# Five channels of a depthwise convolution: the running sum in a PSUM bank instead of SBUF

## The chip, the cores and the metric

The kernel runs on one core of a Trainium2 chip. The core has five engines with a queue each, which run in order and wait for each other through semaphores: TensorE (PE in the profile) multiplies matrices into PSUM, VectorE (DVE) and ScalarE (ACT) work on SBUF and PSUM, GpSimd (POOL) works on SBUF, SyncE (SP) starts most transfers. PSUM is used here as eight banks of 128 partitions by 512 float32 numbers. The metric is the device time of one execution in microseconds (us); before the change it is 1309.3 us, the median of three runs (1308.62 to 1310.32).

## The reference, cut to what matters

A decoder layer on 512 tokens of 1024 features: half of a feed-forward layer, a mixer of attention and convolution, the second half of the feed-forward, and an embedding under a gate. What the change touches is the mixer's convolution branch:

```python
x = x + 0.5 * swiglu(rmsnorm(x, ffn1_norm[i]), ffn1_wgu[i], ffn1_wdown[i])
h = rmsnorm(x, mix_norm[i])
z = h @ w_in[i]
...
a = sliding_window_attention(q, k, v, sinks[i]) @ attn_proj[i]
ca, cb = jnp.split(zc, 2, axis=-1)
u = ca * jax.nn.sigmoid(cb)
u = causal_depthwise_conv(u, dw_w[i], dw_b[i])     # 31 taps, each channel by itself
c = jax.nn.silu(layernorm(u, conv_ln_g[i], conv_ln_b[i])) @ conv_proj[i]
merged = jax.nn.sigmoid(ga) * a + jax.nn.sigmoid(gb) * c
x = x + merged @ w_out[i]
```

For every channel, y[t] = b + the sum over d = 0 to 30 of w[30 − d] · u[t − d].

## The kernel before, in words

Activations lie as [feature, token] tiles of 128 × 512 in float32; the 1024 features are eight such tiles. Every large product is made of float32 operands split into a high and a low part, so each 128 × 128 block of weights costs three matmuls (`mm3`, L113 to L115). A weight arrives as a piece of 512 KB on SyncE's queue; ScalarE rounds it to the high part `whi` (L88) and VectorE subtracts to get `wlo` (L89; for the gates GpSimd does).

The mixer's parts are issued in an order written out by hand, the string ORDER (L39 to L43): `a` and `b` are the convolution's input and gate projections (`ca`, `cb`), `A`, `E`, `V` the scores, softmax and values of one block of 128 queries and eight heads, `g` and `h` the gates' projections (`ga`, `gb`), `p` attention's projection (`ap`), `L` the convolution's norm. From this program order a scheduler makes each engine's queue ahead of time, by priorities and by its own estimate of times. `conv_gate` (L299) makes the convolution's input u (L306) and calls `conv` under `tc.high_priority(offset=-800)`, an offset that puts the taps behind other work that is ready.

"Channel c" below means a tile of 128 channels. `conv` (L311) starts y with the first tap and the bias on VectorE (L314), then adds 30 taps. For c = 0, 2 and 4 ScalarE makes each product `ct` (L322) in a ring of two buffers and GpSimd adds it to y (L323). For c = 1, 3, 5, 6 and 7 VectorE does product and addition in one instruction (L325): y, shifted by d, = u × weight + y; u, y and the weight (one number for each partition) all lie in SBUF. That makes 5 × 30 = 150 instructions in five chains. `conv_norm` (L523) then sums the eight y on GpSimd (L528, L530), takes mean and variance, and normalizes.

The eight PSUM banks are two rings: `pf_tile`, four banks, for the projections and `f_g`; `ps_tile`, 8 − NPF = four banks, for `f_u` of the feed-forward and, in the mixer, for the transposed queries (`qTp`, L411), four tiles of scores per block (`sc`, L430), the transposed probabilities (`pT`, L470), the values' output (`o`, L478), and the norms' column sums and spreads. A tile's bank is free once its last reader is done: for `sc` that is VectorE's mask-and-maximum L438, which also makes the maxima `m`; for `qTp` and `pT` ScalarE's high part (L88) and VectorE's low part (L89, `qT_l`, `p_l`); for `o` four ScalarE copies (L484). L454 is the softmax's exponential on ScalarE, L462 its scaling on GpSimd.

Of the kernel before, what the change touches and what calls it, by code (L numbers as in the profile page):

```python
# [8 lines left out]
F32 = mybir.dt.float32  # L9
# [25 lines left out]

# The order in which the mixer's parts are issued: K keys and values, Q a half of the queries;
# A scores, E softmax, V values of one block; a, b the convolution's input and its gate;
# g, h the gates' projections; p attention's projection; L the convolution's norm.
ORDER = """  # L39
# [7 lines left out]
def hybrid_layer(ctx: ExitStack, tc: tile.TileContext, a: dict, out: bass.AP):  # L47
# [9 lines left out]
    def ps_tile(name):  # L57
        return psum.tile([P, S], F32, tag="ps", name=name, bufs=8 - NPF)

    def pf_tile(name):  # L60
        return psum.tile([P, S], F32, tag="pf", name=name, bufs=NPF)

    def ftile(name):
        return act.tile([P, S], F32, tag="a", name=name, bufs=NBIG)
# [4 lines left out]
    NBIG = 60  # L69
    NPF = 4  # L70

    def ttile(name):
# [11 lines left out]

# [1 line left out]
    def split_into(hi, lo, src, scale=None, eng=nc.vector):  # L86
# [14 lines left out]
    def piece(src, eng=nc.vector):  # L101
        """A weight piece [P, n] from DRAM as its two parts."""
        n = src.shape[1]
        raw = wraw.tile([P, PIECE], F32, tag="raw", name="raw")
        hi = wspl.tile([P, PIECE], F32R, tag="hi", name="whi")
        lo = wspl.tile([P, PIECE], F32R, tag="lo", name="wlo")
        nc.sync.dma_start(raw[:, 0:n], src)
        split_into(hi[:, 0:n], lo[:, 0:n], raw[:, 0:n], eng=eng)
        return hi, lo

    def mm3(ps, w, x, start, stop):
        """ps += w.T @ x of operands in two parts."""
        nc.tensor.matmul(ps, w[1], x[0], start=start, stop=False)  # L113
        nc.tensor.matmul(ps, w[0], x[0], start=False, stop=False)  # L114
        nc.tensor.matmul(ps, w[0], x[1], start=False, stop=stop)  # L115
# [3 lines left out]

# [1 line left out]
    def rsqrt(name, v, n):  # L121
        """1/sqrt(v) of a small positive tile by Newton's iteration."""
        y = small.tile([P, n], F32, tag=f"y{n}", name=f"{name}_y", bufs=2 if n > 8 else 4)
        h = small.tile([P, n], F32, tag=f"h{n}", name=f"{name}_h", bufs=2)
        nc.vector.tensor_single_scalar(
            h.bitcast(I32), v.bitcast(I32), 1, op=ALU.logical_shift_right
        )
        nc.vector.tensor_scalar(
            y.bitcast(I32), h.bitcast(I32), -1, 0x5F3759DF, op0=ALU.mult, op1=ALU.add
        )  # L130
        nc.vector.tensor_scalar(h, v, -0.5, None, op0=ALU.mult)
        for _ in range(3):
            b = small.tile([P, n], F32, tag=f"b{n}", name=f"{name}_b", bufs=2)
            nc.vector.tensor_tensor(b, y, y, op=ALU.mult)
            nc.vector.tensor_tensor(b, b, h, op=ALU.mult)
            nc.vector.scalar_tensor_tensor(y, b, 1.5, y, op0=ALU.add, op1=ALU.mult)
        return y

    def colsum(name, acc):
        """Sums over the partitions of [P, S], tokens on partitions: [P, NT] in PSUM."""  # L140
        ps = ps_tile(f"{name}_cs")
        for t in range(NT):
            nc.tensor.matmul(
                ps[:, t : t + 1], acc[:, t * P : (t + 1) * P], ones[:, 0:1], start=True, stop=True
            )
        return ps[:, 0:NT]
# [7 lines left out]
    def spread(name, r):  # L154
        """[P, NT], tokens on partitions, to [P, S] with tokens on the free axis, on each partition."""
        dg = tmp.tile([P, NT, P], F32, tag="t", name=f"{name}_dg")
        nc.vector.tensor_tensor(
            dg,
            ident.unsqueeze(1).broadcast_to([P, NT, P]),
            r.unsqueeze(2).broadcast_to([P, NT, P]),  # L160
            op=ALU.mult,
        )
        ps = ps_tile(f"{name}_sp")
        nc.tensor.matmul(ps, ones, dg.rearrange("p t q -> p (t q)"), start=True, stop=True)
        rb = tmp.tile([P, S], F32, tag="rb", name=f"{name}_rb", bufs=3)
        nc.scalar.copy(rb, ps)
        return rb
# [16 lines left out]

# [1 line left out]
    g_all = const.tile([P, 8, KD], F32, name="g_all")  # L186
# [23 lines left out]
    def consts():  # L210
# [19 lines left out]

        # the gains of q's and k's unrotated parts are both k's
        qcs, kcs = table("qcs", gq), table("kcs", gk)
# [3 lines left out]
    def ffn(tag, wgu, wdown, h, ss, first, after):  # L236
        """x += 0.5 * swiglu; `after` takes each new tile of x."""
        rb = None
# [45 lines left out]

# [1 line left out]
    def proj(tag, w_piece, h, nk=KD, off=0, bank=None):  # L286
        """One [P, S] tile of h @ w, features on partitions."""
        ps = (bank or pf_tile)(tag)
        for k in range(nk):
            c = off + k * P  # L290
            mm3(ps, part(w_piece, slice(c, c + P)), h[k], k == 0, k == nk - 1)
        return ps
# [16 lines left out]

    # depthwise causal convolution; some channels' taps are ScalarE's and GpSimd's  # L310
    def conv(c):  # L311
        u = us[c]
        ys[c] = y = ftile(f"y{c}")
        nc.vector.tensor_scalar(  # L314
            y, u, dww[:, c, PAD:TAPS], dwb[:, c : c + 1], op0=ALU.mult, op1=ALU.add
        )
        for d in range(1, TAPS):
            wk = dww[:, c, PAD - d : TAPS - d]
            yd, ud = y[:, d:S], u[:, 0 : S - d]
            if c in (0, 2, 4):  # L320
                t = tmp.tile([P, S], F32, tag="ct", name=f"ct{c}_{d}", bufs=2)[:, 0 : S - d]
                nc.scalar.activation(t, ud, AF.Copy, scale=wk)  # L322
                nc.gpsimd.tensor_tensor(yd, yd, t, op=ALU.add)  # L323
            else:
                nc.vector.scalar_tensor_tensor(yd, ud, wk, yd, op0=ALU.mult, op1=ALU.add)  # L325

    # q, k, v with tokens on partitions
    def heads_rsqrt(tag, zs, n, scale):
        """scale / sqrt(mean of squares + EPS) of each head of each block of tokens."""
        v = small.tile([P, NT * n], F32, tag=f"hv{n}", name=f"{tag}_v", bufs=2)  # L330
# [9 lines left out]
    def rope(tag, z3, n, tab, t):  # L340
        """Gain and rotation of the rotated part of each head, in place."""
        w = tmp.tile([P, n, 16], F32, tag="rope", name=f"{tag}_w", bufs=2)
# [7 lines left out]
    def token_major(tag, pieces, kper, n):  # L350
        """h2.T @ w for each block of tokens: NT tiles in PSUM, several to a bank when they are small."""
        per = S // n
# [14 lines left out]
    kT = [rtile(f"kT{i}") for i in range(2)]  # L367
    # each part of v as [v0, 0, v1], so that a pair's heads take their own half of a column
    vp = [act.tile([P, 2, 3, HD], F32R, tag="a", name=f"v{t}", bufs=NBIG) for t in range(NT)]
# [25 lines left out]
    def queries(g):  # L395
        """Four pairs of heads (j, j + 8) of the queries, rotated; their norm and the scores' scale are in rq."""
        pss = token_major(f"q{g}_", [a["wq"][4 * g + i] for i in range(4)], 2, S)
# [11 lines left out]
    def scores(g, t):  # L409
        """Masked scores of eight heads (four pairs) of one block of queries, and their maxima."""  # L410
        pt = ps_tile(f"qTp{g}_{t}")  # L411
# [93 lines left out]
    def attn_proj(o):  # L505
        """Attention's projection under its gate."""
        if o == 0:
# [15 lines left out]
    def conv_norm():  # L523
        """Layer norm over channels, then silu."""
        acc = tmp.tile([P, S], F32, tag="acc", name="ln_acc", bufs=2)
# [48 lines left out]

# [1 line left out]
    h4, ss4, after4 = next_norm("pg", g_gate)  # L576
# [11 lines left out]

# [1 line left out]
    rb4 = None  # L590
# [31 lines left out]
def _layout(inputs):  # L622
    """The inputs as the program reads them, and tables that depend on shapes alone."""
    import numpy as np
# [6 lines left out]
    def kxn(w):  # L631
        """[K, N] -> [N/128 tiles][128 of K, K/128, 128 of N]."""
        kt, nt = w.shape[0] // P, w.shape[1] // P
        return w.reshape(kt, P, nt, P).transpose(2, 1, 0, 3).reshape(nt, P, kt * P)
# [31 lines left out]

    rows = lambda v: np.broadcast_to(v, (P, v.shape[-1]))  # noqa: E731
    gains = np.stack(
# [53 lines left out]
```

## Time and profile before

| | |
|---|---|
| median of three runs | 1309.3 us (1308.62 to 1310.32) |
| span of the profiled execution | 1306.9 us |
| TensorE busy | 1241.3 us (95%) |
| VectorE busy | 804.9 us (62%) |
| ScalarE busy | 496.8 us (38%) |
| GpSimd busy | 379.5 us (29%) |

The profile is one execution. Its page cuts the span into 40 slices of 32.7 us and gives each engine's busy share in tenths (9 is 90% or more); "PEclk" is the clock that TensorE was granted, in tenths of full speed. Groups of instructions are listed as line, engine, operation, output<-inputs, shapes, count | busy us, mean ns | idle us of the engine ahead of them and who ended it. A view of one line gives the shortest, median and longest duration in ns, and the first and last start in us. The chain of waits is followed back from the last instruction to what released each step. A shorter shape stands for a whole group: the taps' widths run from 511 down to 482. In a timeline several instructions of one kind in a row are merged, with their count.

### The profile page before, as it was taken

The numbers are of one execution on the slowest core, as the hardware profiler recorded it, in microseconds if no ns is written. First come the engines' busy times: TensorE is split into PE (matmuls) and PEld (weight loads), VectorE is DVE, ScalarE is ACT, GpSimd is POOL, SyncE is SP. The second block draws the span as 40 slices with busy tenths as digits, with TensorE's granted clock in tenths as the row PEclk, the third lists the DMA queues.
The fourth block names the chain that finished last, engine by engine and source line by source line (L and its number), as shares of the span: only waits on it lengthen the run. The fifth ranks groups of instructions, "written<-read, shape, count | busy, mean of one in ns | idle before, by whom it ended". The sixth has DMA issues, their size and how long they took to land.

```text
span 1306.9 us, 14445 instructions
## 1 busy us (share of the span) xinstructions
PE 1241.3 (95%) x5534; PEld 1015.0 (78%) x5534; DVE 804.9 (62%) x1076; ACT 496.8 (38%) x789; POOL 379.5 (29%) x322
## 2 busy tenths in 40 slices
PE   7999999999999878786889999999999999999998
PEld 5888888888888666565767878888888888888886
DVE  7544444434448988999999665575444444444447
ACT  5333333222225457563755454333333333222242
POOL 4000000011116979867687350050000000011140
PEclk9999999999999989898988999999999999999999
DMA  6223222333322212121011123232232223333331
GB/s 210 97 97 97 97 97 97 89 100 94 101 95 71 80 49 65 49 65 49 17 49 65 65 97 113 81 113 83 97 99 98 95 97 98 96 89 105 109 97 65
DMA packets 35206, 115.27 MB, mean 88 GB/s; under 512 B 4416, under 2 KB 5952, under 8 KB 35136
## 3 DMA queue, kind: packets, MB, share of 16 engines
q1 hardware_dynamic: 34992, 114.31, 27.2%
q8 instruction: 43, 0.70, 0.2%
q14 instruction: 27, 0.22, 0.1%
q10 hardware_dynamic: 144, 0.03, 0.0%
HBM read 112.23 MB, written 2.10 MB: 87 GB/s over the span
## 4 chain that ended last, share of the span: by engine, by line
PE 75%; DVE 18%; ACT 3%; POOL 2%; issue 2%; DMA 0%; SPq 0%; DVEq 0%; POOLq 0%
DVE y L325 10%; PE f_d L114 6%; PE f_d L113 6%; PE f_d L115 6%; PE f_g L115 6%; PE f_u L115 6%; PE f_g L114 6%; PE f_g L113 6%; PE f_u L114 6%; PE f_u L113 6%; DVE wlo L89 2%; POOL y L323 1%; ACT s L454 1%; PE cp L113 1%; PE wo L115 1%
## 5 line engine op out<-in xcount | busy, mean ns | idle before, releaser
L88 ACT ACTIVATE whi<-raw 128x1024 fp32r<-128x1024 f32 (+1 forms) x210 | 219.4, 1045 | 566.9 <-PE f_u L115 258.6
L89 DVE TENSOR_TENSOR wlo<-raw,whi 128x1024 fp32r<-128x1024 f32 (+1 forms) x194 | 258.1, 1331 | 240.6 <-ACT whi L88 240.5
L325 DVE SCALAR_TENSOR_TENSOR y<-u,c_dww,y 128x511 f32<-128x511 f32 (+15 forms) x150 | 171.7, 1156 | 1.4
L323 POOL TENSOR_TENSOR y<-y,ct 128x511 f32<-128x511 f32 (+14 forms) x90 | 127.3, 1415 | 35.0 <-ACT ct L322 29.5
L113 PE MATMUL f_d<-f_a_h,wlo 128*128 128x512 f32 x352 | 137.1, 390 | 0.0
L115 PE MATMUL f_d<-f_a_l,whi 128*128 128x512 f32 x352 | 137.1, 389 | 0.0
L114 PE MATMUL f_d<-f_a_h,whi 128*128 128x512 f32 x352 | 137.1, 389 | 0.0
L257 DVE TENSOR_TENSOR f_gs<-f_g,f_n_rb 128x512 f32<-128x512 f32 x44 | 30.4, 691 | 104.7 <-PE f_g L115 95.9
L322 ACT ACTIVATE ct<-u,c_dww 128x511 f32<-128x511 f32 (+14 forms) x90 | 62.4, 707 | 65.7 <-POOL y L323 65.2
L113 PEld LDWEIGHTS f_d<-f_a_h,wlo 128*128 128x128 f32 x352 | 66.1, 188 | 13.8
L115 PEld LDWEIGHTS f_d<-f_a_l,whi 128*128 128x128 f32 x352 | 66.1, 188 | 13.7
L114 PEld LDWEIGHTS f_d<-f_a_h,whi 128*128 128x128 f32 x352 | 66.1, 188 | 13.6
L180 POOL TENSOR_TENSOR pg_ss_acc<-xt 128x512 f32<-128x512 f32 x1 | 1.0, 1040 | 252.9 <-DVE xt L270 252.9
L180 POOL TENSOR_TENSOR mix_ss_acc<-xt 128x512 f32<-128x512 f32 x1 | 1.0, 1039 | 235.2 <-DVE xt L270 235.2
L113 PE MATMUL f_u<-f_h_h,wlo 128*128 128x512 f32 x176 | 69.0, 392 | 0.0
L113 PE MATMUL f_g<-f_h_h,wlo 128*128 128x512 f32 x176 | 68.7, 390 | 0.0
L115 PE MATMUL f_u<-f_h_l,whi 128*128 128x512 f32 x176 | 68.6, 390 | 0.0
L114 PE MATMUL f_g<-f_h_h,whi 128*128 128x512 f32 x176 | 68.6, 390 | 0.0
L114 PE MATMUL f_u<-f_h_h,whi 128*128 128x512 f32 x176 | 68.6, 390 | 0.0
L115 PE MATMUL f_g<-f_h_l,whi 128*128 128x512 f32 x176 | 68.6, 390 | 0.0
L113 PE MATMUL f_u<-h_h,wlo 128*128 128x512 f32 x168 | 65.9, 392 | 0.0
L115 PE MATMUL f_u<-h_l,whi 128*128 128x512 f32 x168 | 65.5, 390 | 0.0
(320 smaller groups left out, 2883.7 us busy)
## 6 DMA issues: line engine op xcount, KB each, us to landing
raw<-in_wgu SPq DMA_DIRECT2D x86, 512.0 KB, 3.5
raw<-in_wd SPq DMA_DIRECT2D x32, 512.0 KB, 3.6
raw<-in_wzc SPq DMA_DIRECT2D x16, 512.0 KB, 3.5
raw<-in_wzg SPq DMA_DIRECT2D x16, 512.0 KB, 3.4
raw<-in_wd SPq DMA_DIRECT2D x16, 384.0 KB, 3.1
raw<-in_wq SPq DMA_DIRECT2D x8, 512.0 KB, 3.4
raw<-in_wap SPq DMA_DIRECT2D x8, 512.0 KB, 3.5
raw<-in_wcp SPq DMA_DIRECT2D x8, 512.0 KB, 3.4
```

The lines of the kernel that those rows point to most:

```text
L88: nc.scalar.activation(hi, src, AF.Copy)
L89: eng.tensor_tensor(lo, src, hi.bitcast(F32), op=ALU.subtract)
L113: nc.tensor.matmul(ps, w[1], x[0], start=start, stop=False)
L114: nc.tensor.matmul(ps, w[0], x[0], start=False, stop=False)
L115: nc.tensor.matmul(ps, w[0], x[1], start=False, stop=stop)
L180: nc.gpsimd.tensor_tensor(to, v, v, op=ALU.mult)
L257: nc.vector.tensor_tensor(g, pg, rb, op=ALU.mult)
L322: nc.scalar.activation(t, ud, AF.Copy, scale=wk)
L323: nc.gpsimd.tensor_tensor(yd, yd, t, op=ALU.add)
L325: nc.vector.scalar_tensor_tensor(yd, ud, wk, yd, op0=ALU.mult, op1=ALU.add)
L454: nc.scalar.activation(si, si, AF.Exp, bias=nm[:, i : i + 1], accum_out=den[:, i : i + 1])
```

## The change

A third PSUM ring of one bank, `cv`, is taken from the shared ring `ps`, which is left with three. For channels 1, 3, 5, 6 and 7 the first tap (L314) writes into a tile of this bank, the 30 further taps (L325) read and write it in place, and after the last one ScalarE copies it to y in SBUF. Channels 0, 2 and 4 are as before. Apart from this, only comments and documentation strings go.

```diff
     def ps_tile(name):
-        return psum.tile([P, S], F32, tag="ps", name=name, bufs=8 - NPF)
+        return psum.tile([P, S], F32, tag="ps", name=name, bufs=8 - NPF - NCV)
...
+    def cv_tile(name):
+        return psum.tile([P, S], F32, tag="cv", name=name, bufs=NCV)
...
     NPF = 4
+    NCV = 1
...
         ys[c] = y = ftile(f"y{c}")
+        own = c in (0, 2, 4)
+        acc = y if own else cv_tile(f"yc{c}")
         nc.vector.tensor_scalar(
-            y, u, dww[:, c, PAD:TAPS], dwb[:, c : c + 1], op0=ALU.mult, op1=ALU.add
+            acc, u, dww[:, c, PAD:TAPS], dwb[:, c : c + 1], op0=ALU.mult, op1=ALU.add
         )
         for d in range(1, TAPS):
             wk = dww[:, c, PAD - d : TAPS - d]
-            yd, ud = y[:, d:S], u[:, 0 : S - d]
-            if c in (0, 2, 4):
+            yd, ud = acc[:, d:S], u[:, 0 : S - d]
+            if own:
                 t = tmp.tile([P, S], F32, tag="ct", name=f"ct{c}_{d}", bufs=2)[:, 0 : S - d]
                 nc.scalar.activation(t, ud, AF.Copy, scale=wk)
                 nc.gpsimd.tensor_tensor(yd, yd, t, op=ALU.add)
             else:
                 nc.vector.scalar_tensor_tensor(yd, ud, wk, yd, op0=ALU.mult, op1=ALU.add)
+        if not own:
+            nc.scalar.copy(y, acc)
```

## The prediction

> **What bounds the kernel now.** The page's slices come first; its DVE row is VectorE, its PE row TensorE.
>
> ```profile
> span 1306.9 us, 14445 instructions
> ...
> PE   7999999999999878786889999999999999999998
> ...
> DVE  7544444434448988999999665575444444444447
> ...
> PEclk9999999999999989898988999999999999999999
> ```
>
> TensorE is full except in slices 13 to 22, and there VectorE is full and the granted clock falls below 9 tenths. The busy time by stretch (two answers; columns: stretch and length, busy time of PE, PE's weight loads, DVE, ACT, POOL with instruction counts, granted clock, DMA share, GB/s) puts edges on it:
>
> ```profile
> 0.00:414.00 414.00, 405.11 (x1823) 335.30 (x1824) 203.43 (x263) 130.27 (x172) 48.32 (x68) 1.00 0.33 106
> 414.00:717.60 303.60, 254.21 (x1141) 200.00 (x1140) 289.10 (x430) 174.12 (x371) 241.96 (x205) 0.90 0.16 51
> 717.60:1306.90 589.30, 582.00 (x2574) 479.64 (x2572) 312.32 (x385) 192.38 (x247) 89.18 (x50) 1.00 0.29 95
> ```
> ```profile
> 414.00:450.00 36.00, 33.02 (x142) 26.82 (x140) 35.47 (x30) 18.09 (x25) 33.93 (x26) 0.95 0.18 59
> 450.00:500.00 50.00, 39.33 (x178) 31.12 (x176) 40.81 (x83) 28.20 (x70) 38.83 (x41) 0.86 0.13 43
> 500.00:550.00 50.00, 41.65 (x195) 32.03 (x196) 48.95 (x74) 29.81 (x59) 48.85 (x50) 0.93 0.20 64
> 550.00:600.00 50.00, 44.82 (x203) 34.80 (x201) 48.58 (x76) 30.95 (x72) 35.25 (x30) 0.93 0.18 56
> 600.00:650.00 50.00, 36.15 (x167) 29.36 (x168) 47.87 (x84) 26.59 (x67) 33.55 (x25) 0.83 0.12 40
> 650.00:717.60 67.60, 59.25 (x262) 45.88 (x261) 67.42 (x88) 40.49 (x81) 51.56 (x37) 0.90 0.15 50
> ```
>
> Outside 414 to 717.6 us TensorE idles 414.0 − 405.1 + 589.3 − 582.0 = 16.2 us in all, at full clock; nothing done to VectorE can shorten those parts by more. Inside, TensorE idles 303.6 − 254.2 = 49.4 us, and VectorE is busy 289.1 of 303.6 us (95%). Multiplying TensorE's busy time by the granted clock, slice by slice (33.02 × 0.95 + 39.33 × 0.86 + 41.65 × 0.93 + 44.82 × 0.93 + 36.15 × 0.83 + 59.25 × 0.90), gives 229 us: the stage's matmul work if it ran unbroken at full clock. So 303.6 − 229 = 75 us is the most that this stage can give.
>
> TensorE's own waits between 430 and 720 us (what waited, for whom, total us, times, longest), then two of the other engines':
>
> ```profile
> PE sc L113 <- DVE m L438: 17.8, 6, 8.2
> PE sc L113 <- DVE qT_l L89: 9.1, 2, 7.5
> ...
> PE pT L472 <- DVE m L438: 5.0, 5, 1.8
> ```
> ```profile
> ACT ct L322 <- POOL y L323: 59.4, 38, 4.8
> ...
> POOL ln_acc L530 <- DVE y L325: 7.1, 1, 7.1
> ```
>
> These three waits for VectorE make 31.9 us. What VectorE does meanwhile is the convolution: the chain of waits over 414 to 718 us gives L325 41.7%, by far its largest item.
>
> ```profile
> by line: DVE y L325 41.7%; DVE wlo L89 7.3%; issue 6.3%; POOL y L323 6.0%; ACT s L454 5.6%; DVE s L438 4.4%; POOL s L462 3.9%; DVE p_l L89 3.4%; DVE q_b L135 1.5%; PE pT L472 1.3%; DVE q_y L136 1.2%; DVE q_b L134 1.2%; ACT ct L322 1.1%; DVE
> L325 DVE SCALAR_TENSOR_TENSOR y<-u,c_dww,y x150: 692/908/2855, 415.5 to 716.8; 128x511 f32<-128x511 f32 x5, 128x510 f32<-128x510 f32 x5, 128x509 f32<-128x509 f32 x5, 128x508 f32<-128x508 f32 x5
> L325 DVE SCALAR_TENSOR_TENSOR y<-u,c_dww,y 128x511 f32<-128x511 f32 (+15 forms) x150 | 171.7, 1156 | 1.4
> ```
>
> **The taps of five channels (150 instructions).** Shortest, median and longest are 692, 908 and 2855 ns, the mean 1156: one operation of nearly one size with a fourfold spread. The timelines of VectorE and of GpSimd (start, length) show why.
>
> ```profile
> 589.56 0.73 DVE L325 SCALAR_TENSOR_TENSOR y<-u,c_dww,y 128x500 f32<-128x500 f32 x1
> 590.21 0.68 DVE L302 TENSOR_TENSOR sg<-cb,mix_n_rb 128x512 f32<-128x512 f32 x1
> ...
> 593.30 7.32 DVE L325 SCALAR_TENSOR_TENSOR y<-u,c_dww,y 128x497 f32<-128x497 f32 x4
> 600.55 0.68 DVE L89 TENSOR_TENSOR qT_l<-qTp,qT_h 128x512 fp32r<-128x512 f32 x1
> ```
> ```profile
> 592.91 2.72 POOL L323 TENSOR_TENSOR y<-y,ct 128x482 f32<-128x482 f32 x2
> 595.58 2.84 POOL L89 TENSOR_TENSOR wlo<-raw,whi 128x1024 fp32r<-128x1024 f32 x1
> 598.39 1.70 POOL L304 TENSOR_TENSOR sg<-sg,mix_n_rb 128x512 f32<-128x512 f32 x1
> 600.06 1.70 POOL L530 TENSOR_TENSOR ln_acc<-ln_acc,y 128x512 f32<-128x512 f32 x1
> ```
>
> While GpSimd runs its own four two-tensor operations (592.91 to 600.09), four taps take 7.32 us, one beside each; yet qT_l at 600.55, which reads its source from PSUM, takes 0.68 us right beside GpSimd's L530. The groups bear it out: with one tensor in PSUM, VectorE's mean is the undisturbed one all through this stage.
>
> ```profile
> L302 DVE TENSOR_TENSOR sg<-cb,mix_n_rb 128x512 f32<-128x512 f32 x8 | 5.5, 682 | 3.0 <-PE cb L115 3.0
> L270 DVE SCALAR_TENSOR_TENSOR xt<-f_d,xt 128x512 f32<-128x512 f32 x16 | 11.1, 692 | 27.4 <-PE f_d L115 27.4
> L261 DVE TENSOR_TENSOR f_us<-f_us,f_gs 128x512 f32<-128x512 f32 x44 | 30.2, 687 | 0.1
> ```
>
> So with the sum in PSUM a tap has one SBUF tensor left (u), and I take 0.72 us for it: between L270's 0.692 and the undisturbed 0.73 above. No row has VectorE writing to PSUM. The bounds are 0.69 us (the shortest tap) and 1.16 us (no gain, if it were disturbed all the same). Saved: 150 × (1.156 − 0.72) = 65 us of VectorE's time, between 0 and 70. VectorE's stage work falls from 289 to 224 us. [...]
>
> [...]
>
> **GpSimd's side.** Its 90 additions for the other three channels lose a competitor.
>
> ```profile
> L323 POOL TENSOR_TENSOR y<-y,ct 128x511 f32<-128x511 f32 (+14 forms) x90 | 127.3, 1415 | 35.0 <-ACT ct L322 29.5
> L180 POOL TENSOR_TENSOR mix_ss_sq<-xt x7: 1039/1040/1041, 284.6 to 374.3; 128x512 f32<-128x512 f32 x7
> ```
>
> Left alone, such an addition takes 1.04 us, so at most 90 × 0.375 = 34 us of GpSimd's time. GpSimd is busy 242 of 303.6 us and 6.0% of the chain, so I count none of it beyond what the forecast below contains.
>
> **First taps and copies.** The first tap (L314) loses nothing that matters: five of
>
> ```profile
> L314 DVE TENSOR_SCALAR y<-u,c_dww,g_all x8: 537/548/1295, 413.1 to 642.2; 128x512 f32<-128x512 f32 x8
> L166 ACT COPY ln_m_rb<-ln_m_sp 128x512 f32<-128x512 f32 x1 | 0.6, 587 | 5.9 <-PE ln_m_sp L164 5.9
> ```
>
> go from 0.54 or 1.3 us to some 0.7: within 1 us either way. ScalarE gains five copies out of PSUM, 5 × 0.59 = 2.9 us, in a stage where it is busy 174 of 303.6 us: hidden in ScalarE's idle time. The new wait is that one bank serves five channels: the first tap of channels 3, 5, 6 and 7 waits for the copy of the one before. That copy may stand in ScalarE's queue behind a ct product that waits for GpSimd (longest 4.8 us). VectorE runs in order, so behind a held first tap stand the mask-and-maximum of the scores (L438), the weight splits wlo and the p_l splits, and TensorE waits for all three. Bounds: 0 to 4 × (4.8 + 0.6) = 22 us of VectorE. The first taps' places can be chosen at scheduling time after the copy, so I take 4 us. GpSimd's channel sum (L530) waits one copy longer at the end, 0.6 us; TensorE has attention's projections then, and is full after 717.6.
>
> **The bank.** The shared ring goes from four to three. In the feed-forward layers one f_u tile fills while the one before drains; each fills over a whole step of 48 matmuls and is read out by one VectorE product of 0.69 us like L261's: two banks would do, so nothing. In the stage, attention turns the ring: 8 blocks with 1 qTp tile, 4 sc tiles and 1 o tile, and 28 pT tiles, 76 in all. A burst of four scores that had four banks now finds its fourth occupied until two L438 have run.
>
> ```profile
> L438 DVE CUSTOM_DVE_ANT_0 s<-sc,c_masks,sk x64: 363/533/548, 472.5 to 671.2; 128x256 f32<-128x256 f32 x48, 128x128 f32<-128x128 f32 x16
> L89 DVE TENSOR_TENSOR p_l<-pT,p_h 128x512 fp32r<-128x512 f32 x28 | 18.8, 678 | 3.1 <-ACT p_h L88 3.1
> ```
>
> That is some 1.1 us a burst, and as much for a burst of pT (one split, 0.68 us, and its ScalarE half): 16 × 1.1 = 18 us at most if nothing covers it and nothing stands ahead in VectorE's queue. Projection matmuls (ca, cb, ga) are issued among them and cover most. I take 5 us; the far end is in the rivals.
>
> **The sum.** VectorE's 65 us do not all become time, because TensorE needs 229 us and attention's chain of scores, softmax and transposes is not VectorE's alone. Its share of full rate is now 229 / 303.6 = 0.75. The stage's own better slices show what it reaches when fed: 550 to 600 has 44.82/50 × 0.93 = 0.83, 414 to 450 has 33.02/36 × 0.95 = 0.87. The stage would then last 229 / 0.83 = 276 or 229 / 0.87 = 263 us, a gain of 28 or 41. VectorE would be at 224 / 263 = 85% or less, so it allows the better one, and I take 41, then subtract the bank's 5 and half of the first taps' 4 (the other half lies in slack): 34 us. The profiled execution would go from 1306.9 to 1272.9 us; the median of the runs, 1309.3, is 2.4 above that span, so the forecast is 1275.3, say 1275 us. About 0.2% (2.6 us) is what a measurement can tell from no change.
>
> **The rivals.**
> - All of VectorE's time becomes the kernel's. For: 95% busy, 41.7% of the chain. Against: it needs TensorE at 229 / (303.6 − 60) = 94% of full rate, which no slice of the stage has. 60 us less: 1249.
> - The wait moves to ScalarE and GpSimd. For: with VectorE emptied, the exponentials (L454, 5.6% of the chain), the scaling L462 (3.9%) and L323 (6.0%) are late next. If TensorE rises only to 0.79 (the last slice: 59.25/67.6 × 0.90), the stage lasts 290: 14 us less, 1295.
> - PSUM access is dearer than the rows show, because writing back to the bank costs time. At 0.9 us a tap VectorE saves 38 us instead of 65, and in proportion the gain is 20: 1289. [...]
> - The lost bank decides, and the kernel is slower. The present wait of sc for m, 17.8 us in 6, is already 3 us each with four banks. If each of the 16 bursts of sc and pT stood 3 us, uncovered, that is 48 us against 41 won plus 4 for first taps: 11 slower, 1320. It decides from 2.3 us a burst. Against: those 3 us are largely taps queued ahead on VectorE, and they become shorter.
> - The change doesn't do what it says: taps in PSUM are disturbed as before (the tap's weight, too, comes from SBUF). Then only bank and waits remain, 7 to 9 us: 1317. Against: L438 reads PSUM with its mask and scalars in SBUF, and its longest of 64 is 548 ns against a median of 533.
>
> **How the numbers follow.** Forecast 0.58; all converted 0.12; moved wait 0.11; dearer PSUM 0.06; bank 0.09; disturbed as before 0.04. The likeliest case itself spans 1260 to 1290 (1309.3 less 41, and less 28 − 7 = 21, with some 8 us at the low end for a new issue order). The range 1249 to 1300 leaves out the last two cases (0.13) and half of the first rival (0.06). Faster: the first four, 0.87, less 0.01 for a moved wait that eats everything: 0.86. Same: that 0.01 and half of the last case, 0.03. Slower: the bank and the rest of the last case, 0.11.
>
> **What would show it.** Right: L325's mean near 0.72 us with a longest under 1 us; L323 nearer 1.1 to 1.3; VectorE's stage work near 225 us; TensorE's idle time in the stage from 49 towards 25 us and the granted clock up; the rest unchanged. Wrong: L325 still over 1 us (no relief), L314 held for the copies, waits of sc or pT for m and p_l that grow, or a stage as long as now with VectorE partly idle.

## The result and the profile after

The changed kernel takes 1353.0 us (median of four runs, 1352.2 to 1354.3) against 1309.4: the ratio is 1.0335, with a 95% interval of 1.0322 to 1.0348. It is 43.6 us slower where 34 us faster was forecast. One execution of the kernel with three shared banks, further down, took 2763 us where its others took 1321 to 1324, and is left out of its figures. The profiled execution's span is 1350.4 us, 43.5 more than before. The changed kernel's lines are shifted: the tap L325 is L332 there, GpSimd's addition L323 is L330, the split L89 is L93, the scores' maximum L438 is L447; the new copy is L334.

The page's slices, the same rows as shown of before:

```profile
PE   7999999999997793994449999999999999999998
...
DVE  7444444444458667566874465565544444344447
...
PEclk9999999999999895997669999999999999999999
```

VectorE is nowhere full any more, and TensorE has holes down to three and four tenths, with a granted clock down to five tenths. The same by stretch, cut where the changed kernel has done about as much of the matmul work as the old one had at 717.6 us (1128 instructions against 1141):

```profile
0.00:414.00 414.00, 405.23 (x1826) 335.45 (x1827) 203.80 (x263) 130.12 (x171) 49.68 (x68) 1.00 0.33 106
414.00:759.10 345.10, 247.20 (x1128) 195.46 (x1128) 232.81 (x433) 182.76 (x378) 195.97 (x206) 0.84 0.14 46
759.10:1350.40 591.30, 584.04 (x2583) 481.18 (x2581) 307.75 (x381) 192.30 (x247) 83.63 (x49) 1.00 0.29 94
```

The first part is as before, and the last within 2 us of what it was. All but these 2 us of the loss lie in the mixer's stage, which went from 303.6 to 345.1 us. VectorE's work in it fell from 289.1 to 232.8 us and GpSimd's from 242.0 to 196.0, while TensorE's idle time grew from 49.4 to 345.1 − 247.2 = 97.9 us. The taps did what the change meant them to do (the view of the line, then its group and GpSimd's):

```profile
L332 DVE SCALAR_TENSOR_TENSOR yc<-u,c_dww,yc x150: 724/739/756, 414.1 to 701.6; 128x511 f32<-128x511 f32 x5, 128x510 f32<-128x510 f32 x5, 128x509 f32<-128x509 f32 x5, 128x508 f32<-128x508 f32 x5
```
```profile
L330 POOL TENSOR_TENSOR y<-y,ct 128x511 f32<-128x511 f32 (+14 forms) x90 | 109.2, 1214 | 20.8 <-ACT ct L329 14.2
L332 DVE SCALAR_TENSOR_TENSOR yc<-u,c_dww,yc 128x511 f32<-128x511 f32 (+9 forms) x150 | 110.8, 739 | 4.7
```

From 692/908/2855 ns (shortest, median, longest) the tap went to 724/739/756: the disturbance is gone, and 61 us of VectorE's time with it. What TensorE waited for is the news:

```profile
PE sc L117 <- DVE qT_l L93: 43.5, 3, 23.5
PE gb L117 <- DVE sga L500: 18.9, 1, 18.9
PE ca L117 <- ACT zq L409: 15.8, 1, 15.8
PE pT L481 <- DVE p_l L93: 14.3, 2, 13.8
```

Those four sum to 92.5 us, in seven waits of which the longest takes 23.5. The first is for data, the low part of the queries. In the others TensorE waits for a bank whose reader is late: VectorE's sga reads the bank of ga, ScalarE's zq those of the queries, VectorE's p_l that of an earlier pT. Two of these three are in the ring of four that the change left alone, and the wait that the lost bank was feared to lengthen, sc for m, is 0.6 us now. So the question is why the readers are late. One wait, in the timelines of VectorE, ScalarE and TensorE:

```profile
642.81 0.19 DVE L465 RECIPROCAL den<-den 128x8 f32<-128x8 f32 x1
642.94 23.22 DVE L332 SCALAR_TENSOR_TENSOR yc<-u,c_dww,yc 128x511 f32<-128x511 f32 x30
667.31 0.69 DVE L93 TENSOR_TENSOR qT_l<-qTp,qT_h 128x512 fp32r<-128x512 f32 x1 [1.15 <-ACT qT_h L92]
```
```profile
648.74 1.06 ACT L92 ACTIVATE whi<-raw 128x1024 fp32r<-128x1024 f32 x1 [4.74 <-PE ga L119]
666.19 0.58 ACT L334 COPY y<-yc 128x512 f32<-128x512 f32 x1 [16.39 <-DVE yc L332]
666.67 0.60 ACT L92 ACTIVATE qT_h<-qTp 128x512 fp32r<-128x512 f32 x1
```
```profile
668.05 0.58 PE L117 MATMUL sc<-kT,qT_l 64*128 64x256 f32 x1 [19.35 <-DVE qT_l L93]
```

All 30 taps of channel 6 stand in VectorE's queue in one piece. Before, the longest such piece was eight:

```profile
415.46 12.65 DVE L325 SCALAR_TENSOR_TENSOR y<-u,c_dww,y 128x511 f32<-128x511 f32 x8
```

The split qT_l of the next block stands behind the 30 taps. ScalarE's copy of the sum stands in ScalarE's queue ahead of the same block's qT_h and holds it for 16.4 us. TensorE, which runs in order too, idles 19.35 us at the block's scores. Channel 7 shows the same (26 taps in 20.06 us from 682.27, then sga, for which gb waits 18.9 us). These two waits have only taps ahead of them, and the copy that waits for the taps.

In the three other long ones (15.8, 23.5 and 13.8 us) products ct of the other channels stand ahead as well, in ScalarE's queue: 10, 15 and 5 in a row, where before the change six was the most. Ahead of the longest of these waits, on VectorE and on ScalarE:

```profile
511.83 15.35 DVE L332 SCALAR_TENSOR_TENSOR yc<-u,c_dww,yc 128x501 f32<-128x501 f32 x20
529.13 0.69 DVE L93 TENSOR_TENSOR qT_l<-qTp,qT_h 128x512 fp32r<-128x512 f32 x1 [1.95 <-ACT qT_h L92]
```
```profile
527.43 0.70 ACT L329 ACTIVATE ct<-u,c_dww 128x483 f32<-128x483 f32 x1 [0.42 <-POOL y L330]
528.03 0.57 ACT L334 COPY y<-yc 128x512 f32<-128x512 f32 x1
528.50 0.60 ACT L92 ACTIVATE qT_h<-qTp 128x512 fp32r<-128x512 f32 x1
```

The 20 taps are done at 527.18 us. The block's qT_h comes only at 528.50, behind fifteen products in a row (from 509.95 on) and a copy. So "order", below, means both queues: VectorE's taps alone are shown for 38 us of the waits, taps and products together for 53.

### The profile page after: what moved, and what is told of

Its sections match the earlier page's. It is cut to its first block, busy times and chain, and to the rows that moved or that the text cites. A ratio compares the mean times of both kernels' runs of the same rounds, so it can differ in the third digit from the quotient of the medians.

```text
span 1350.4 us, 14475 instructions
## 1 busy us (share of the span) xinstructions
PE 1236.5 (92%) x5534; PEld 1012.1 (75%) x5534; DVE 744.4 (55%) x1076; ACT 505.2 (37%) x796; POOL 329.3 (24%) x322
## 4 chain that ended last, share of the span: by engine, by line
PE 85%; DVE 6%; ACT 4%; POOL 4%; issue 1%; DMA 0%; SPq 0%; DVEq 0%; POOLq 0%
PE f_d L117 6%; PE f_d L119 6%; PE f_d L118 6%; PE f_g L117 6%; PE f_u L118 6%; PE f_g L118 6%; PE f_u L117 6%; PE f_g L119 6%; PE f_u L119 6%; DVE yc L332 4%; POOL y L330 3%; PE ca L117 1%; PE gb L117 1%; PE ca L119 1%; PE ca L118 1%; PE gb L118 1%
## 5 line engine op out<-in xcount | busy, mean ns | idle before, releaser
L93 DVE TENSOR_TENSOR wlo<-raw,whi 128x1024 fp32r<-128x1024 f32 (+1 forms) x194 | 255.2, 1316 | 255.9 <-ACT whi L92 255.9
L330 POOL TENSOR_TENSOR y<-y,ct 128x511 f32<-128x511 f32 (+14 forms) x90 | 109.2, 1214 | 20.8 <-ACT ct L329 14.2
L332 DVE SCALAR_TENSOR_TENSOR yc<-u,c_dww,yc 128x511 f32<-128x511 f32 (+9 forms) x150 | 110.8, 739 | 4.7
L261 DVE TENSOR_TENSOR f_gs<-f_g,f_n_rb 128x512 f32<-128x512 f32 x44 | 30.4, 691 | 104.8 <-PE f_g L119 95.9
L119 PEld LDWEIGHTS f_d<-f_a_l,whi 128*128 128x128 f32 x352 | 66.1, 188 | 13.8
L118 PE MATMUL f_u<-h_h,whi 128*128 128x512 f32 x168 | 65.4, 389 | 0.0
L118 PE MATMUL f_g<-h_h,whi 128*128 128x512 f32 x168 | 65.4, 389 | 0.0
```

The costliest lines, as they stand in the source:

```text
L93: eng.tensor_tensor(lo, src, hi.bitcast(F32), op=ALU.subtract)
L261: nc.vector.tensor_tensor(g, pg, rb, op=ALU.mult)
```

## The experiments

Three causes were to be told apart: the **order** (taps in unbroken pieces in VectorE's queue, and with them the other channels' products in ScalarE's, which no run changes apart), the **bank** (three shared banks instead of four), and the **copy** (ScalarE standing for the sum). All ratios are to the kernel before.

**Bank alone.** The kernel before with `bufs=8 - NPF` cut to `7 - NPF`.

```diff
-        return psum.tile([P, S], F32, tag="ps", name=name, bufs=8 - NPF)
+        return psum.tile([P, S], F32, tag="ps", name=name, bufs=7 - NPF)
```

> The kernel before (sums in SBUF), with the shared PSUM ring cut from four banks to three and nothing else. Order theory (the loss comes from taps that stand in VectorE's queue in unbroken runs ahead of attention's steps): the bank alone costs little, 1309 to 1318 us. Bank theory (three shared banks throttle attention): 1335 us or more, TensorE waiting for m and p_l.

Ratio 1.010 (1.0083 to 1.0117): 13 us slower. That is between the two expectations, a fair part of the loss but less than a third of it. The profile comes from a further run.

> The kernel before with three shared banks once more, for a profile of it: 1320 to 1324 us. If the bank costs by holding the scores and transposes, TensorE's waits of sc, pT and o for m, p_l and p_h add up to more than the 43 us of the kernel before by about 10; if it costs by a worse order, VectorE's queue shows longer stretches of taps instead.

One run, 1325.0 us. TensorE's waits:

```profile
PE sc L113 <- DVE m L438: 18.1, 11, 5.9
PE sc L113 <- DVE qT_l L89: 13.6, 3, 6.0
```

sc waits for m eleven times instead of six, but for the same sum (18.1 against 17.8 us); qT_l costs 4.5 us more, and small waits of the projections, such as ga for u with 4.0 us, make up some of the rest. Neither expectation is met: the waits that the first one names add up to 38 us instead of 43, and the longest piece of taps is eight as before. That the bank costs 13 us is shown; by which path stays open.

**A finishing copy without PSUM.** Sums in SBUF in a tile of their own, copied at the chain's end by ScalarE; all four shared banks.

```diff
-        return psum.tile([P, S], F32, tag="ps", name=name, bufs=8 - NPF - NCV)
+        return psum.tile([P, S], F32, tag="ps", name=name, bufs=8 - NPF)
...
-        acc = y if own else cv_tile(f"yc{c}")
+        acc = y if own else ftile(f"yc{c}")
```

> Sums in SBUF in a tile of their own, copied by ScalarE at the chain's end, four shared banks: the finishing copy without PSUM. Order theory: VectorE's queue has the same unbroken runs as the changed kernel, and the taps are disturbed by GpSimd besides, so 1350 us or more, up to 1400. Bank theory: no bank is lost, 1309 to 1315. Copy theory (only ScalarE standing for the copy costs): 1340 to 1355.

1391.3 us, ratio 1.0629 (1.0614 to 1.0645): 82 us slower with no bank lost. Its taps take 1078 ns in the mean, disturbed as before the change, and TensorE's wait of sc for qT_l grew further:

```profile
PE sc L117 <- DVE qT_l L93: 59.9, 2, 36.8
```

VectorE's queue has the pieces again, up to all 30 taps of a channel, and this with four shared banks:

```profile
719.07 25.51 DVE L332 SCALAR_TENSOR_TENSOR yc<-u,c_dww,yc 128x511 f32<-128x511 f32 x30
```

The order theory's number; the bank theory is out as the main cause.

**The same with the copies issued later.** As the last one, but the five copies are issued in `conv_norm`.

```diff
-        if not own:
-            nc.scalar.copy(y, acc)
+        accs[c] = None if own else acc
...
         for c in range(KD):
+            if accs[c] is not None:
+                nc.scalar.copy(ys[c], accs[c])
```

> Sums in SBUF in tiles of their own, four shared banks, as in the run with the finishing copies at the chains' ends (1391 us), but the five ScalarE copies are issued with the convolution's norm. Order theory: the taps stand scattered in VectorE's queue as before the change, so 1309 to 1318 us. If the separate tile or the copy itself were what costs: 1340 or more.

1315.7 us, ratio 1.0047 (1.0033 to 1.0062). Same instructions, same tiles, taps no less disturbed (mean 1170 ns); only the place of five copies in the program differs, and with it the order that the scheduler makes. The longest piece of taps is eight again:

```profile
652.55 8.37 DVE L334 SCALAR_TENSOR_TENSOR yc<-u,c_dww,yc 128x497 f32<-128x497 f32 x8
```

The difference is 1391.3 − 1315.7 = 75.6 us. It lies in the order theory's range and rules out the separate tile and the copy as such.

**No ScalarE copy.** The changed kernel, with the last tap reading the bank and writing y in SBUF.

```diff
+        taps = list(range(1, TAPS)) if own else list(range(2, TAPS)) + [1]
...
-                nc.vector.scalar_tensor_tensor(yd, ud, wk, yd, op0=ALU.mult, op1=ALU.add)
+                to = y[:, d:S] if d == 1 else yd
+                nc.vector.scalar_tensor_tensor(to, ud, wk, yd, op0=ALU.mult, op1=ALU.add)
...
-            nc.scalar.copy(y, acc)
+            nc.vector.tensor_copy(y[:, 0:1], acc[:, 0:1])
```

> The changed kernel, but the last tap of a channel reads the bank and writes y in SBUF itself, with one column copied by VectorE, so ScalarE has no copy. Order theory: the unbroken runs remain, qT_l and p_l still stand behind them, 1330 to 1355 us. Copy theory: ScalarE no longer stands, 1275 to 1300. Bank theory: 1345 to 1353.

1353.8 us, ratio 1.0338 (1.0321 to 1.0356): not to be told from the changed kernel. Its timelines of VectorE and ScalarE at channel 6 show why:

```profile
645.09 22.43 DVE L334 SCALAR_TENSOR_TENSOR yc<-u,c_dww,yc 128x510 f32<-128x510 f32 x29
667.55 0.75 DVE L334 SCALAR_TENSOR_TENSOR y<-u,c_dww,yc 128x511 f32<-128x511 f32 x1
668.22 0.15 DVE L336 COPY y<-yc 128x1 f32<-128x1 f32 x1
668.28 0.68 DVE L93 TENSOR_TENSOR qT_l<-qTp,qT_h 128x512 fp32r<-128x512 f32 x1
```
```profile
651.06 0.58 ACT L92 ACTIVATE qT_h<-qTp 128x512 fp32r<-128x512 f32 x1
```

qT_h now runs at 651.06, 15 us sooner than in the changed kernel, and it helps nothing: qT_l still stands behind 29 taps until 668.28. ScalarE's long wait for the taps was real, but without it the time is the same. The copy theory is out. The fifteen products in a row are still there in this version, so they are not ruled out as a part of the order's price.

**The order put right.** PSUM sums, one bank for them, three shared, ScalarE's copies; but `conv` only fills a list, and `tick` takes taps from it into the program between the mixer's other steps: two after a weight piece, one after each bank of scores and after each split of pT, and the rest at `conv_norm`. `begin` is the first tap, into the bank. The priority offset around `conv` goes too, so the other channels' products also move: at most six of them stand in a row now.

```diff
+    def tick(n):
+        for _ in range(min(n, len(todo))):
+            todo.pop(0)()
...
+        todo.append(begin)
+        todo.extend(lambda d=d: tap(d) for d in range(1, TAPS))
+        todo.append(lambda: nc.scalar.copy(y, box[0]))
...
+        tick(2)
```

> The changed kernel's PSUM sums, one bank for them, three shared ones, ScalarE's copies, but the taps are put into program order a few at a time between the mixer's other steps (one or two after each weight piece, score pair and probability split) instead of as one block. Order theory: the forecast gain comes back, 1262 to 1290 us. Bank theory: 1335 or more. Copy theory: 1290 to 1320, since the copies stay in ScalarE's queue.

1293.6 us, ratio 0.9876 (0.9862 to 0.9891): 1.2% faster than the kernel before. That is 3.6 us above the order theory's range and inside the copy theory's, which the run without copies had ruled out. Its stretches:

```profile
414.00:702.00 288.00, 272.05 (x1246) 216.39 (x1245) 235.96 (x430) 185.65 (x389) 198.26 (x204) 0.93 0.19 63
702.00:1291.60 589.60, 561.20 (x2463) 461.51 (x2461) 304.55 (x384) 184.46 (x234) 82.92 (x50) 0.97 0.28 90
```

TensorE idles only 16 us in the stage, but 28 us behind it, where it was 7: the taps came too late (the last starts at 717 us), and the norm behind them held TensorE. That asks for taps issued sooner.

**Sooner.** `tick` with 3, 1 and 2 (piece, bank of scores, split), then with 3, 2 and 3, then with 4, 2 and 4.

> The paced version with the taps issued sooner: three after each weight piece, one after each score pair, two after each probability split. The taps should end some 10 us earlier, so the norm holds TensorE less after 702 us: 1275 to 1292 us. Rival, that pacing has nothing more to give because the lost bank sets the rest: 1293 again.

> The paced version with the taps issued sooner still: three after each weight piece, two after each score pair, three after each probability split; the partner in PSUM of the run with pacing alone. 1268 to 1290 us if ending the taps sooner frees the norm; 1293 to 1305 if the denser taps again stand ahead of attention's steps.

> The paced version with four taps after each weight piece, two after each score pair, four after each probability split. If sooner is still better: 1268 to 1273. If the taps begin to stand ahead of attention's steps again (one stretch of fifteen in VectorE's queue): 1276 to 1285.

1276.2 us (0.9747, 0.9732 to 0.9761), 1274.6 us (0.9738, 0.9723 to 0.9752) and 1292.7 us (0.9874, 0.9859 to 0.9890). The first two lie in their ranges, the last above both of its expectations. It has one stretch of fifteen in VectorE's queue, and TensorE behind it:

```profile
662.63 11.47 DVE L346 SCALAR_TENSOR_TENSOR yc<-u,c_dww,yc 128x496 f32<-128x496 f32 x15
674.01 0.68 DVE L547 TENSOR_TENSOR sgb<-gb,mix_n_rb 128x512 f32<-128x512 f32 x1
```
```profile
674.84 0.77 PE L121 MATMUL gb<-mix_h_h,wlo 128*128 128x512 f32 x1 [9.84 <-DVE sgb L547]
675.40 0.63 PE L122 MATMUL gb<-mix_h_h,whi 128*128 128x512 f32 x1
...
679.67 0.54 PE L123 MATMUL gb<-mix_h_l,whi 128*128 128x512 f32 x1
680.04 0.39 PE L121 MATMUL gb<-mix_h_h,wlo 128*128 128x512 f32 x1
680.27 0.40 PE L122 MATMUL gb<-mix_h_h,whi 128*128 128x512 f32 x1
```

That is the order theory in small, but not all of the 18 us. Before the stretch begins this version is already some 11 us late: the 978 matmuls that the version of 1274.6 us does from 414 to 644.1 us take it until 654.9. And the version of 1276.2 us has a stretch of thirteen, with a wait of TensorE behind it about as long, and is fast all the same:

```profile
667.39 9.91 DVE L346 SCALAR_TENSOR_TENSOR yc<-u,c_dww,yc 128x494 f32<-128x494 f32 x13
PE ap L121 <- ACT oT_h L92: 10.5, 1, 10.5
```

Of the other 11 us, one wait of 8.4 us falls into that time, of o for ScalarE's p_h; the rest stays open.

**Pacing without PSUM.** The version of 1274.6 us with the sum in y in SBUF, no copy and four shared banks.

```diff
-            box.append(cv_tile(f"yc{c}"))
+            box.append(y)
...
-        todo.append(lambda: nc.scalar.copy(y, box[0]))
```

> Pacing alone: the taps issued three after each weight piece, two after each score pair, three after each probability split, but with the sum in y in SBUF, no copy and four shared banks. If PSUM's undisturbed taps make the gain: 1305 to 1330 us, L325's mean still over 1 us. Rival, that the pacing by itself made the gain of the paced version: 1275 to 1295.

1315.0 us, ratio 1.0044 (1.0030 to 1.0058). Pacing gains nothing by itself, 5.6 us slower than the kernel before; with the taps in PSUM the same program is 1315.0 − 1274.6 = 40.4 us faster, though it pays for the bank and the copies. The tap's group in the two, SBUF and PSUM:

```profile
L346 DVE SCALAR_TENSOR_TENSOR y<-u,c_dww,y 128x496 f32<-128x496 f32 (+18 forms) x150 | 163.2, 1098 | 1.6
```
```profile
L346 DVE SCALAR_TENSOR_TENSOR yc<-u,c_dww,yc 128x511 f32<-128x511 f32 (+9 forms) x150 | 110.1, 734 | 2.3
```

**Paced, without the copies.** The version of 1274.6 us with the last tap writing y, as above.

> The paced version of 1274.6 us, with the last tap writing y in SBUF itself and VectorE copying one column, so that ScalarE has no copies of the sums. If the copies hold ScalarE or the single bank's turn holds VectorE: 1268 to 1272 us. If they are hidden: 1273 to 1277.

1281.9 us, ratio 0.9788 (0.9771 to 0.9806): 7 us slower than with the copies, which neither expectation had. The copies are not what is left to win. Where the 7 us went stays open; this program's queue is another one again, and more than that hung on the queue elsewhere.

## Why the prediction was wrong

**Right, with its size.** The tap's price: 0.72 us expected, 0.739 measured, with a longest of 756 ns where under 1 us was asked. VectorE's stage work: 224 expected, 232.8 measured. GpSimd's addition: 1.1 to 1.3 us expected, 1.214 measured. A tap with one tensor in SBUF was not disturbed by GpSimd in the changed kernel: the 20 taps from 511.83 us on took 724 to 745 ns each while GpSimd was busy 14.41 of the 15.35 us, where before the change four taps beside GpSimd's operations took 7.32 us; all 150 lie within 32 ns of each other (724 to 756). What the sum in PSUM adds to a tap is small: at equal width the shortest tap went from 706 to 724 ns (482 columns) and from 739 to 755 ns (511 columns).

One reading was looser than the text had it. Of the three rows with which it showed undisturbed means "all through this stage", L270 and L261 run in the feed-forward layers, where GpSimd is nearly idle (48.3 of the first 414 us), and L261 has no tensor in PSUM; only L302 has instructions in the stage, six of its eight, at 680 ns.

**The step that failed.** It is the sum. It took TensorE's rate in the stage's better slices, 0.83 and 0.87, as what TensorE reaches "when fed", and so took for granted that VectorE's queue would go on feeding it: taps scattered in pieces of one to eight among the splits and maxima that attention waits for. For a new order of the queues it allowed "some 8 us" at the low end, as a further gain, and nothing on the slow side. In the changed kernel the queue is another: taps in pieces of up to 30. An emptier engine is no help to one who stands behind 23 us of its work. The order by itself costs 75.6 us with the sums in SBUF and four banks (1391.3 against 1315.7). With the sums, the bank and the copies of the changed kernel, breaking up the pieces, of taps and of products, wins 1353.0 − 1274.6 = 78.4 us. The order ate the gain of the taps and 43 us more. What came is the last of the prediction's signs of being wrong, "a stage as long as now with VectorE partly idle".

**Mis-sized.** The bank was put at 5 us and costs 13 alone. The rival that had the bank decide had the right sign for the wrong reason: the waits of sc for m, which it extrapolated, sank from 17.8 to 0.6 us.

**The wait seen from the wrong side.** The text had VectorE held at a first tap by a copy late in ScalarE's queue. It was ScalarE that stood for taps, 16.4 us at channel 6 alone, while VectorE idled 0.1 us in all ahead of its five first taps. Neither decided: the version without copies takes the same time as the changed kernel.

**What held after all.** With the taps scattered by hand the forecast's mechanism gives 1274.6 us; forecast were 1275. That it agrees to the microsecond is luck: the taps in PSUM won 40.4 us there, net of bank and copies, where 34 were reckoned, and the pacing itself cost 5.6 us (1315.0 against 1309.4, in SBUF), where nothing was.

**Open.** Why the scheduler strings the taps together was not settled. Shown is what switches it: finishing the sum into another tile right behind the chain does (by ScalarE's copy, with the sum in PSUM or in SBUF, or by the last tap, with the sum in PSUM), and issuing the copies with the norm doesn't (with the sum in SBUF). What its estimates or priorities do in between no run shows. Nor does a run part the taps in VectorE's queue from the products in ScalarE's. Late copies with PSUM sums weren't tried: five sums would need five banks.

## What to carry to other kernels

Where a scheduler makes the queues, an edit that is to make instructions cheaper can also move them, here by what finishes the chain: before pricing the edit, ask what the queue will be, and compare the two orders ahead of the times. Fill-in work belongs in small portions between the steps that another engine waits for; 15 in a row cost TensorE a wait of 10 us here, 30 in a row one of 19. And five VectorE accumulations beside a busy GpSimd were worth a PSUM bank. By an estimate, the 40.4 us that they won net and the bank's own 13 make some 11 us a chain, so one chain alone would not pay for the bank; no run has fewer than five.

## What the runs showed of the hardware that was not expected

The first tap, which has one tensor input, is dearer into PSUM: 813 ns against 544 undisturbed into SBUF (the groups of the changed kernel):

```profile
L321 DVE TENSOR_SCALAR yc<-u,c_dww,g_all 128x512 f32<-128x512 f32 x5 | 4.1, 813 | 0.1
L321 DVE TENSOR_SCALAR y<-u,c_dww,g_all 128x512 f32<-128x512 f32 x3 | 1.6, 544 | 0.1
```

And a wait cost TensorE more than its length: after the 9.84 us of the version with 4, 2 and 4, the matmuls shown above take 0.63 instead of 0.39 us, starting 0.43 instead of 0.23 us apart, for the 5.2 us up to 680.04. Twelve matmuls begin in that time where at 0.23 us some 23 would. The granted clock (third column from the end) is half of full speed in that time and full behind it:

```profile
674.00:680.00 6.00, 5.16 (x12) 4.13 (x13) 3.32 (x6) 4.49 (x7) 1.28 (x1) 0.50 0.00 0
680.00:690.00 10.00, 10.00 (x51) 8.20 (x51) 3.44 (x6) 5.09 (x11) 2.40 (x1) 1.00 0.01 2
```
